# Two matmuls instead of three in each step of a recursive SwiGLU product, and weight sums made by DMA

## The chip, the cores and the metric

The kernel runs on one core of a Trainium2 chip. The metric is device time in microseconds (us) of one execution. Engines are named as in the profile: PE (matrix multiply), PEld (its weight loads), DVE (elementwise), ACT (activations and copies), POOL, and SP, whose queue issues most DMAs here.

## The reference, cut to what matters

One encoder layer on 512 tokens of width 2048, in float32: a gated linear attention mixer, a SwiGLU feed-forward block of width 5632, a gated input embedding and a last norm. The change touches only the first product of the feed-forward block:

```python
def swiglu(hn, w_in, w_out):
    gate, up = jnp.split(jnp.einsum('btd,de->bte', hn, w_in), 2, axis=-1)
    return jnp.einsum('btf,fd->btd', jax.nn.silu(gate) * up, w_out)
```

Here `w_in` is 2048 x 11264: 5632 columns of gate, then 5632 of up.

## The kernel before, in words

**Stages.** Activations lie with features on the 128 partitions and 512 tokens along the row. Four stages follow each other: the mixer (to about 714 us of the span), its output product (to 858 us), gate and up (864 to 1756 us), the down product and the embedding (to the end). All the large products run on PE in a split form: each float32 operand is cut into a high part (rounded by an ACT copy to the matmul type) and a low part (the rest, by a DVE subtraction), and a product is high by high, high by low and low by high, three matmuls that add into the same PSUM tile.

**Gate and up.** For each of 44 column tiles n (128 columns of gate and the 128 columns of up beside them) the kernel needs a 2 x 2 block product: weights a11, a12 (gate, upper and lower half of the 2048 input features) and a21, a22 (up), against two token halves of 256. It uses a seven-product recursive scheme: products p1, p2, p3, p4, q5, q6, p7, each of 8 steps of 128 features. The forms of the activations (`FM`) are made once. The forms of the weights are made for every n: a11, a12, a22 themselves, S3 = a11 + a21 for p7, s1 = a21 + a22 for q5, a11 + s1 for q6, and a12 + (a11 + s1) for p3. Results add up in three PSUM tiles, R1 (p1, q6, q5, p3), R2 (p2) and R7 (p7, p4); `combine` takes intermediate copies (v1, v2, v4) and builds gate `g` and up `u`, which are multiplied and written to memory by a DMA of POOL (`f_mid`).

**Order.** The stream for one n is p1(n), p3(n-1), p2(n), p7(n), q6(n), p4(n-1), q5(n). Raw weights are loaded (`Form.load`) five entries of the stream ahead, and a form is made (`Form.prep`: the sums, then high and low) two entries ahead. A scheduler then orders the instructions of each engine; each engine works through its own list in that order. High parts have three buffers, low parts three, raw weights six (`wr`): a load into one of these six has to wait until the last reader of what lay there is done.

**Names.** Every DVE and ACT operation is issued by one helper, line 70, so they are told apart by tiles: `w_hi` and `w_lo` are the parts of a form, `w_a` a raw weight tile, `w_s` (w_s3) the sum S3. Lines 724, 725 and 726 are the three matmuls, lines 123 to 125 the three matmuls of the other stages, line 676 the load of raw weights, line 761 the write of `f_mid`.

Of the kernel before, what the change touches and what calls it, by code (L numbers as in the profile page):

```python
# [9 lines left out]
F32 = mybir.dt.float32  # L10
F32R = mybir.dt.float32r
U8 = mybir.dt.uint8
AF = mybir.ActivationFunctionType
ALU = mybir.AluOpType

P = 128
T = 512
# [14 lines left out]
TH = T // 2  # L32
KH = KT // 2
# [4 lines left out]
def hybrid_kernel(ctx, tc, xT, pT, w_wide, w_lr, w_gu, b_gate, gla_norm, w_out,  # L38
                  mix_norm, ffn_norm, w_ffn_in, w_ffn_out, ple_norm, w_ple, fin_norm,
                  masks, resets, fold, outT):  # L40
    nc = tc.nc
    const = ctx.enter_context(tc.tile_pool(name="const", bufs=1))
    pp = ctx.enter_context(tc.tile_pool(name="pp", bufs=16))
    wp = ctx.enter_context(tc.tile_pool(name="wp", bufs=2))
# [4 lines left out]
    def f(ap):  # L49
        return ap.bitcast(F32)  # L50

    def bank(name):
        return mm_ps.tile([P, T], F32, name=name, tag="mm")
# [19 lines left out]
    vec = Counted(nc.vector, 60)  # L73
    act = Counted(nc.scalar, 100)
# [14 lines left out]
    WMAX = 8 * P  # L89

    class Block:
# [4 lines left out]
        def prep(self):  # L96
            if self.hi is not None:
                return
            n, m = self.n, self.m
            raw = wp.tile([P, WMAX], F32, name="w_raw", tag="raw", bufs=2)[:, : n * m]  # L100
            nc.sync.dma_start(raw.rearrange("p (k m) -> p k m", m=m), self.src)
            hi = wp.tile([P, WMAX], F32R, name="w_hi", tag="whi", bufs=3)[:, : n * m]
            lo = wp.tile([P, WMAX], F32R, name="w_lo", tag="wlo", bufs=3)[:, : n * m]
            act.activation(hi, raw, AF.Copy)
            vec.tensor_tensor(lo, raw, f(hi), ALU.subtract)
            self.hi = hi.rearrange("p (k m) -> p k m", m=m)
            self.lo = lo.rearrange("p (k m) -> p k m", m=m)
# [539 lines left out]
    rstd2 = wr = None  # L647
# [8 lines left out]
        out_ctx.close()  # L656
        wr = wr_ctx.enter_context(tc.tile_pool(name="wr", bufs=6))

    RAWS = {"p1": "a11", "p2": "a12", "p7": "a21", "q6": "a22"}
    FORM = {"p1": 1, "p2": 2, "p3": 3, "p4": 4, "q5": 5, "q6": 6, "p7": 7}  # L660
    pairs = {}

    class Form:
# [4 lines left out]
            self.w = pairs.setdefault(n, {})  # L668

        def load(self):  # L670
            name = RAWS.get(self.kind)
            if name is None or self.loaded or wr is None:
                return
            self.loaded = True
            t = wr.tile([P, WMAX], F32, name="w_a", tag="raw")
            nc.sync.dma_start(t.rearrange("p (k m) -> p k m", m=P), self.src(name))
            self.w[name] = t

        def prep(self):
            if self.hi is not None or wr is None:  # L680
                return
            self.load()
            w, kind = self.w, self.kind
            if kind == "p7":
                w["s3"] = wp.tile([P, WMAX], F32, name="w_s3", tag="raw", bufs=2)
                vec.tensor_tensor(w["s3"], w["a11"], w["a21"], ALU.add)
            elif kind == "q6":
                vec.tensor_tensor(w["a21"], w["a21"], w["a22"], ALU.add)
                vec.tensor_tensor(w["a11"], w["a11"], w["a21"], ALU.add)
            elif kind == "p3":  # L690
                vec.tensor_tensor(w["a12"], w["a12"], w["a11"], ALU.add)
            raw = w[{"p1": "a11", "p2": "a12", "p3": "a12", "p4": "a22", "q5": "a21", "q6": "a11", "p7": "s3"}[kind]]
            hi = wp.tile([P, WMAX], F32R, name="w_hi", tag="whi", bufs=3)
            lo = wp.tile([P, WMAX], F32R, name="w_lo", tag="wlo", bufs=3)
            act.activation(hi, raw, AF.Copy)
            vec.tensor_tensor(lo, raw, f(hi), ALU.subtract)
            self.hi = hi.rearrange("p (k m) -> p k m", m=P)
            self.lo = lo.rearrange("p (k m) -> p k m", m=P)
# [3 lines left out]
    def flush():  # L702
        while pending:
            pending.pop(0)()

    def product(b):
        b.prep()
        w, kind = b.w, b.kind
        if kind == "p1":
            w["R1"] = bank("ps_r1")  # L710
        elif kind == "p2":
            w["R2"] = bank("ps_r2")
        elif kind == "p7":
            w["R7"] = bank("ps_r7")
        ps = w[{"p2": "R2", "p7": "R7", "p4": "R7"}.get(kind, "R1")][:, 0:TH]
        fm = FM[FORM[kind]]
        fresh = kind in ("p1", "p2", "p7")
        if (b.n, kind) in ((0, "q5"), (FT - 1, "p3")):
            flush()
        for k in range(KH):  # L720
            xh, xl = fm[k][:, 0, :], fm[k][:, 1, :]
            ah, al = b.hi[:, k, :], b.lo[:, k, :]
            go = dict(skip_group_check=True)
            nc.tensor.matmul(ps, ah, xh, start=fresh and k == 0, stop=False, **go)  # L724
            nc.tensor.matmul(ps, ah, xl, start=False, stop=False, **go)  # L725
            nc.tensor.matmul(ps, al, xh, start=False, stop=k == KH - 1, **go)  # L726
        flush()
        pending.append(lambda: combine(b, ps))

    def temp(name):  # L730
        return pp.tile([P, T], F32, name=name, tag="res")

    A_T, B_T = slice(0, TH), slice(TH, T)

    def combine(b, ps):
        w, kind = b.w, b.kind
        if kind == "p1":
            w["v1"] = temp("v1")[:, A_T]
            act.activation(w["v1"], ps, AF.Copy)
        elif kind == "p2":  # L740
            g = w["g"] = temp("g")
            vec.tensor_tensor(g[:, A_T], ps, w["v1"], ALU.add)
            vec.tensor_tensor(g[:, A_T], g[:, A_T], rstd2[:, A_T], ALU.mult)
        elif kind == "q6":
            w["v2"] = temp("v2")[:, A_T]
            act.activation(w["v2"], ps, AF.Copy)
        elif kind == "q5":
            v4 = temp("v4")[:, A_T]
            act.activation(v4, ps, AF.Copy)
            w["u"] = temp("u")  # L750
            vec.tensor_tensor(w["u"][:, B_T], w["R7"][:, 0:TH], v4, ALU.subtract)
        elif kind == "p3":
            g = w["g"]
            vec.tensor_tensor(g[:, B_T], ps, rstd2[:, B_T], ALU.mult)
            act.activation(g, g, AF.Silu)
            vec.tensor_tensor(g, g, rstd2, ALU.mult)
        elif kind == "p4":
            u = w["u"]
            vec.tensor_tensor(u[:, A_T], ps, w["v2"], ALU.subtract)
            vec.tensor_tensor(u, u, w["g"], ALU.mult)  # L760
            nc.gpsimd.dma_start(Fd[b.n], u)
            pairs[b.n] = None
# [8 lines left out]
    for n in range(FT + 1):  # L771
        for kind, i in (("p1", n), ("p3", n - 1), ("p2", n), ("p7", n), ("q6", n), ("p4", n - 1), ("q5", n)):
            if 0 <= i < FT:
                stream.append((Form(i, kind, ffn_block(i)),
                               (lambda b: late_b(b)) if n == 0 else product))

    def late_b(b):

        product(b)
        at = ("p1", "p2", "p7", "q6").index(b.kind) if b.kind != "q5" else None  # L780
        if at is not None:
            for j in range(2 * at, 2 * at + 2):
                late_forms_b(j)
# [148 lines left out]
    for m in range(KT - LAST, KT):  # L932
        kept[m] = []
        for k0 in range(0, KT + PT, 4):
            k1 = min(k0 + 4, KT + PT)
            b = KeptBlock(ple_src(m, k0, k1), k1 - k0, P, "w")
# [90 lines left out]
    for m in range(KT - LAST, KT):  # L1027
        ps = bank("ps_hb")
# [91 lines left out]
```

## Time and profile before

| | us |
|---|---|
| median of 3 runs | 2457.65 (2456.04 to 2458.02) |
| the profiled execution | 2453.24 |
| its span, first to last instruction | 2451.4 |
| gate and up, in the span | 863.5 to 1756 |

The profile gives, for each engine, its busy time and, in the timeline, the start and length of each instruction. Lengths of matmuls overlap: the next one starts before the one before has left the array, so the rate is read from the distance between starts, not from the length. The same holds in a smaller way for DVE and ACT. "To landing" of a DMA is the time from its issue to its last byte.

### The profile page before, as it was taken

What the parts mean: (1) busy time and instruction counts of PE and PEld (TensorE: products, weight loads), DVE (VectorE), ACT (ScalarE), POOL (GpSimd) and SP (SyncE); (2) the same over time, 40 slices, a digit from 0 to 9 for tenths busy, and PEclk for the clock granted to TensorE, in tenths of its full rate; (3) what the DMA queues carried; (4) which work ended last, traced back from release to release, by engine and by line L of the source; (5) the groups of instructions that cost most, each with busy time, mean ns of one, the idle gap of its engine ahead of it and who ended that gap; (6) DMA issues with size and microseconds to landing.
All of it is one profiled execution on the core that took longest, in us unless ns stands there. A gap on an engine that the chain in (4) does not pass through costs nothing.

```text
span 2451.4 us, 35287 instructions
## 1 busy us (share of the span) xinstructions
PE 2410.5 (98%) x14428; PEld 2150.6 (88%) x14428; DVE 1596.6 (65%) x2220; ACT 1040.4 (42%) x1352; POOL 50.7 (2%) x102
## 2 busy tenths in 40 slices
PE   9999999999999999999999999999999999999997
PEld 6788887887888789999999999999888888888887
DVE  7595875856964487878787877878642422345445
ACT  5554644545543354444444444444431311234333
POOL 0000000000000000000000000000000000000000
PEclk9999999999999999999999999999999999999999
DMA  6222222222234243333333333333574644433333
GB/s 198 81 78 73 78 72 80 84 64 86 67 127 155 99 142 117 117 117 117 119 122 121 118 117 117 117 117 117 201 265 148 198 142 146 114 97 97 97 97 114
DMA packets 98099, 289.92 MB, mean 118 GB/s; under 512 B 12048, under 2 KB 17296, under 8 KB 97936
## 3 DMA queue, kind: packets, MB, share of 16 engines
q1 hardware_dynamic: 90576, 263.54, 34.3%
q0 software_dynamic: 7360, 24.12, 2.5%
q8 instruction: 113, 1.85, 0.3%
q14 instruction: 50, 0.41, 0.1%
HBM read 259.31 MB, written 28.31 MB: 117 GB/s over the span
## 4 chain that ended last, share of the span: by engine, by line
PE 95%; DVE 2%; ACT 2%; issue 1%; DMA 0%; SPq 0%; DVEq 0%; ACTq 0%
PE ps_r L724 12%; PE ps_r L725 12%; PE ps_r L726 12%; PE ps_dn L124 7%; PE ps_dn L125 7%; PE ps_dn L123 6%; PE ps_qk L123 2%; PE ps_qk L125 2%; PE ps_qk L124 2%; PE ps_out L124 2%; PE ps_og L123 2%; PE ps_out L125 2%; PE ps_out L123 2%; PE ps_og L124 2%; PE ps_og L125 2%; PE ps_pg L125 2%
## 5 line engine op out<-in xcount | busy, mean ns | idle before, releaser
L70 DVE TENSOR_TENSOR w_lo<-w_raw,w_hi 128x1024 fp32r<-128x1024 f32 (+2 forms) x271 | 306.4, 1131 | 352.2 <-ACT w_hi L70 351.8
L70 ACT ACTIVATE w_hi<-w_raw 128x1024 fp32r<-128x1024 f32 (+2 forms) x271 | 266.3, 983 | 613.2 <-PE ps_dn L124 303.7
L70 ACT ACTIVATE w_hi<-w_a 128x1024 fp32r<-128x1024 f32 x264 | 280.1, 1061 | 425.2 <-PE ps_r L725 298.4
L70 DVE TENSOR_TENSOR w_lo<-w_a,w_hi 128x1024 fp32r<-128x1024 f32 x264 | 322.4, 1222 | 104.7 <-ACT w_hi L70 98.5
L724 PE MATMUL ps_r<-fme,w_hi 128*128 128x256 f32 x1056 | 300.6, 285 | 5.2 <-issue 4.8
L725 PE MATMUL ps_r<-fme,w_hi 128*128 128x256 f32 x1056 | 300.3, 284 | 0.0
L726 PE MATMUL ps_r<-fme,w_lo 128*128 128x256 f32 x1056 | 299.9, 284 | 0.0
L123 PE MATMUL ps_dn<-hlf,w_hi 128*128 128x512 f32 x704 | 273.9, 390 | 1.6 <-ACT hlf L70 1.6
L124 PE MATMUL ps_dn<-hlf,w_hi 128*128 128x512 f32 x704 | 274.2, 389 | 0.4 <-DVE hlf L70 0.4
L125 PE MATMUL ps_dn<-hlf,w_lo 128*128 128x512 f32 x704 | 274.1, 389 | 0.0
L724 PEld LDWEIGHTS ps_r<-fme,w_hi 128*128 128x128 f32 x1056 | 204.1, 193 | 6.3 <-issue 5.6
L725 PEld LDWEIGHTS ps_r<-fme,w_hi 128*128 128x128 f32 x1056 | 204.1, 193 | 0.0
L726 PEld LDWEIGHTS ps_r<-fme,w_lo 128*128 128x128 f32 x1056 | 203.8, 193 | 0.0
L724 PE MATMUL ps_r<-fmb,w_hi 128*128 128x256 f32 x704 | 199.5, 283 | 1.3 <-ACT v L70 1.3
L724 PE MATMUL ps_r<-fma,w_hi 128*128 128x256 f32 x704 | 199.5, 283 | 0.0
L726 PE MATMUL ps_r<-fma,w_lo 128*128 128x256 f32 x704 | 199.4, 283 | 0.0
L725 PE MATMUL ps_r<-fmb,w_hi 128*128 128x256 f32 x704 | 199.4, 283 | 0.0
L725 PE MATMUL ps_r<-fma,w_hi 128*128 128x256 f32 x704 | 199.4, 283 | 0.0
L726 PE MATMUL ps_r<-fmb,w_lo 128*128 128x256 f32 x704 | 199.4, 283 | 0.0
L70 DVE TENSOR_TENSOR w_a<-w_a 128x1024 f32<-128x1024 f32 x132 | 160.9, 1219 | 20.6 <-DMA w_a<-in_w_ffn_in_dram 20.4
L123 PEld LDWEIGHTS ps_dn<-hlf,w_hi 128*128 128x128 f32 x704 | 132.1, 188 | 29.0 <-ACT hlf L70 1.8
L124 PEld LDWEIGHTS ps_dn<-hlf,w_hi 128*128 128x128 f32 x704 | 132.2, 188 | 28.2 <-DVE hlf L70 0.9
(244 smaller groups left out, 5089.1 us busy)
## 6 DMA issues: line engine op xcount, KB each, us to landing
w_a<-in_w_ffn_in_dram SPq DMA_DIRECT2D x176, 512.0 KB, 3.6
w_raw<-in_w_wide_dram SPq DMA_DIRECT2D x95, 512.0 KB, 3.5
w_raw<-in_w_ffn_out_dram SPq DMA_DIRECT2D x64, 512.0 KB, 3.7
w_raw<-in_w_ple_dram SPq DMA_DIRECT2D x42, 384.0 KB, 3.1
w_raw<-in_w_out_dram SPq DMA_DIRECT2D x24, 512.0 KB, 3.7
h<-h_mid SPq DMA_DIRECT2D x48, 256.0 KB, 3.8
w_raw<-in_w_ffn_out_dram SPq DMA_DIRECT2D x32, 384.0 KB, 3.2
f_mid<-u POOLq DMA_DIRECT2D x44, 256.0 KB, 3.6
```

Source lines behind the costliest of these rows:

```text
L70: return getattr(self.engine, op)(out, *args, **kw)
L123: nc.tensor.matmul(ps, ah, bh, start=first, stop=False)
L124: nc.tensor.matmul(ps, ah, bl, start=False, stop=False)
L125: nc.tensor.matmul(ps, al, bh, start=False, stop=last)
L724: nc.tensor.matmul(ps, ah, xh, start=fresh and k == 0, stop=False, **go)
L725: nc.tensor.matmul(ps, ah, xl, start=False, stop=False, **go)
L726: nc.tensor.matmul(ps, al, xh, start=False, stop=k == KH - 1, **go)
```

## The change: 512 columns at once, and sums by DMA

High by high and high by low have the same weights (the high part), and the high and low part of the activations lie side by side. The two matmuls of 256 columns become one of 512, into both halves of the PSUM tile; low by high is added into the second half. So the wanted value is the sum of the two halves, and `combine` now works on 512 columns and adds the halves at the end (`merge`; in p3 an ACT copy and a DVE addition). Two of the four weight sums, S3 and s1, are no longer added by DVE: a plain load brings the first summand and a second DMA, issued by POOL, adds the other one into the same tile. For this a11, a21 and a22 are read from memory twice. S3 lies in the two-buffer pool that held it before; s1, a11, a12 and a22 share the six.

```diff
-    RAWS = {"p1": "a11", "p2": "a12", "p7": "a21", "q6": "a22"}
+    RAWS = {"p1": ("a11",), "p2": ("a12",), "p7": ("a21", "a11"), "q6": ("a21", "a22"), "p4": ("a22",)}
+    KEEP = {"p1": "a11", "p2": "a12", "p7": "s3", "q6": "s1", "p4": "a22"}
+    SPLIT = {"p1": "a11", "p2": "a12", "p3": "a12", "p4": "a22", "q5": "s1", "q6": "a11", "p7": "s3"}
...
-            t = wr.tile([P, WMAX], F32, name="w_a", tag="raw")
-            nc.sync.dma_start(t.rearrange("p (k m) -> p k m", m=P), self.src(name))
-            self.w[name] = t
+            pool, bufs = (wp, 2) if self.kind == "p7" else (wr, 6)
+            t = pool.tile([P, WMAX], F32, name="w_a", tag="raw", bufs=bufs)
+            nc.sync.dma_start(t, self.src(names[0]).rearrange("p k m -> p (k m)"))
+            for more in names[1:]:
+                nc.gpsimd.dma_start(t, self.src(more).rearrange("p k m -> p (k m)"), accum_op=ALU.add)
+            self.w[KEEP[self.kind]] = t
...
-            if kind == "p7":
-                w["s3"] = wp.tile([P, WMAX], F32, name="w_s3", tag="raw", bufs=2)
-                vec.tensor_tensor(w["s3"], w["a11"], w["a21"], ALU.add)
-            elif kind == "q6":
-                vec.tensor_tensor(w["a21"], w["a21"], w["a22"], ALU.add)
-                vec.tensor_tensor(w["a11"], w["a11"], w["a21"], ALU.add)
+            if kind == "q6":
+                vec.tensor_tensor(w["a11"], w["a11"], w["s1"], ALU.add)
...
-            nc.tensor.matmul(ps, ah, xh, start=fresh and k == 0, stop=False, **go)
-            nc.tensor.matmul(ps, ah, xl, start=False, stop=False, **go)
-            nc.tensor.matmul(ps, al, xh, start=False, stop=k == KH - 1, **go)
+            nc.tensor.matmul(ps, b.hi[:, k, :], fm[k].rearrange("p a x -> p (a x)"),
+                             start=fresh and k == 0, stop=False, **go)
+            nc.tensor.matmul(ps[:, TH:T], b.lo[:, k, :], fm[k][:, 0, :], start=False, stop=k == KH - 1, **go)
...
+    def merge(out, t):
+        vec.tensor_tensor(out, t[:, A_T], t[:, B_T], ALU.add)
...
         if kind == "p1":
-            w["v1"] = temp("v1")[:, A_T]
+            w["v1"] = temp("v1")
             act.activation(w["v1"], ps, AF.Copy)
         elif kind == "p2":
             g = w["g"] = temp("g")
-            vec.tensor_tensor(g[:, A_T], ps, w["v1"], ALU.add)
-            vec.tensor_tensor(g[:, A_T], g[:, A_T], rstd2[:, A_T], ALU.mult)
+            vec.tensor_tensor(w["v1"], ps, w["v1"], ALU.add)
+            merge(g[:, A_T], w["v1"])
...
-            vec.tensor_tensor(w["u"][:, B_T], w["R7"][:, 0:TH], v4, ALU.subtract)
+            vec.tensor_tensor(v4, w["R7"], v4, ALU.subtract)
+            merge(w["u"][:, B_T], v4)
         elif kind == "p3":
             g = w["g"]
-            vec.tensor_tensor(g[:, B_T], ps, rstd2[:, B_T], ALU.mult)
+            act.activation(g[:, B_T], ps[:, B_T], AF.Copy)
+            vec.tensor_tensor(g[:, B_T], ps[:, A_T], g[:, B_T], ALU.add)
+            vec.tensor_tensor(g, g, rstd2, ALU.mult)
             act.activation(g, g, AF.Silu)
             vec.tensor_tensor(g, g, rstd2, ALU.mult)
         elif kind == "p4":
             u = w["u"]
-            vec.tensor_tensor(u[:, A_T], ps, w["v2"], ALU.subtract)
+            vec.tensor_tensor(w["v2"], ps, w["v2"], ALU.subtract)
+            merge(u[:, A_T], w["v2"])
```

On PE, at the start of p1 of column tile 22, two of the eight steps stood like this before (ps_r1 is R1, fme a form of the activations):

```order
L724 MATMUL ps_r1_11646<-fme_5615,w_hi_11578 128x256
L725 MATMUL ps_r1_11646<-fme_5615,w_hi_11578 128x256
L726 MATMUL ps_r1_11646<-fme_5615,w_lo_11579 128x256
L724 MATMUL ps_r1_11646<-fme_5615,w_hi_11578 128x256
L725 MATMUL ps_r1_11646<-fme_5615,w_hi_11578 128x256
L726 MATMUL ps_r1_11646<-fme_5615,w_lo_11579 128x256
```

And with the change (two steps and the first matmul pair of the next, which has another tile of forms):

```order
L724 MATMUL ps_r1_10538<-fme_5615,w_hi_10482 128x512
L726 MATMUL ps_r1_10538<-fme_5615,w_lo_10483 128x256
L724 MATMUL ps_r1_10538<-fme_5615,w_hi_10482 128x512
L726 MATMUL ps_r1_10538<-fme_5615,w_lo_10483 128x256
L724 MATMUL ps_r1_10538<-fme_5828,w_hi_10482 128x512
L726 MATMUL ps_r1_10538<-fme_5828,w_lo_10483 128x256
```

A step is one matmul of 512 columns and one of 256 instead of three of 256; the order of the products is the same.

On DVE, from the low part of p1(22) to the low part of q6(22), the list before reads (w_a_11478 is a11 of tile 22, 11576 a21, 11608 a22, 11546 a12, w_s3 the sum S3; 11317 is a12 of tile 21):

```order
L70 TENSOR_TENSOR w_lo_11579<-w_a_11478,w_hi_11578 128x1024
L70 TENSOR_TENSOR w_a_11576<-w_a_11576,w_a_11608 128x1024
L70 TENSOR_TENSOR u_11444<-ps_r7_11289,v2_11377 128x256
L70 TENSOR_TENSOR w_lo_11612<-w_a_11317,w_hi_11611 128x1024
L70 TENSOR_TENSOR u_11444<-u_11444,g_11314 128x512
L70 TENSOR_TENSOR w_a_11478<-w_a_11478,w_a_11576 128x1024
L70 TENSOR_TENSOR w_lo_11643<-w_a_11546,w_hi_11642 128x1024
L70 TENSOR_TENSOR u_11673<-ps_r7_11518,v4_11671 128x256
L70 TENSOR_TENSOR w_a_11546<-w_a_11546,w_a_11478 128x1024
L70 TENSOR_TENSOR w_lo_11678<-w_s3_11675,w_hi_11677 128x1024
L70 TENSOR_TENSOR g_11543<-ps_r1_11417,rstd2_6615 128x256
L70 TENSOR_TENSOR w_lo_11712<-w_a_11478,w_hi_11711 128x1024
```

With the change the same stretch reads (w_a_10404 is a11 of tile 22, 10504 the loaded and added s1, 10479 S3, 10457 a12, 10279 a12 of tile 21):

```order
L70 TENSOR_TENSOR w_lo_10483<-w_a_10404,w_hi_10482 128x1024
L70 TENSOR_TENSOR w_a_10404<-w_a_10404,w_a_10504 128x1024
L70 TENSOR_TENSOR v2_10324<-ps_r7_10259,v2_10324 128x512
L70 TENSOR_TENSOR w_lo_10509<-w_a_10279,w_hi_10508 128x1024
L70 TENSOR_TENSOR u_10379<-v2_10324 128x256
L70 TENSOR_TENSOR u_10379<-u_10379,g_10276 128x512
L70 TENSOR_TENSOR w_lo_10535<-w_a_10457,w_hi_10534 128x1024
L70 TENSOR_TENSOR v4_10555<-ps_r7_10437,v4_10555 128x512
L70 TENSOR_TENSOR w_a_10457<-w_a_10457,w_a_10404 128x1024
L70 TENSOR_TENSOR u_10557<-v4_10555 128x256
L70 TENSOR_TENSOR w_lo_10561<-w_a_10479,w_hi_10560 128x1024
L70 TENSOR_TENSOR w_lo_10586<-w_a_10404,w_hi_10585 128x1024
```

The sum for q6 (second row) stands where the sum s1 stood, and reads the tile that the adding DMA fills; the low part of q6 (last row) is the last reader of a11, and in the six-buffer rotation the tile s1 of column tile 23 takes the place of a11 of tile 22.

On POOL, around the write of tile 21, only writes stood before:

```order
L761 DMA f_mid20_134<-u_11444 128x512
L761 DMA f_mid21_135<-u_11673 128x512
L761 DMA f_mid22_136<-u_11902 128x512
```

and with the change (10835 is S3 of tile 24, 10682 is s1 of tile 23, 11013 S3 of 25, 10860 s1 of 24; the L682 rows are adding DMAs):

```order
L769 DMA f_mid20_134<-u_10379 128x512
L682 DMA w_a_10835<-in_w_ffn_in_dram 128x1024
L682 DMA w_a_10682<-in_w_ffn_in_dram 128x1024
L769 DMA f_mid21_135<-u_10557 128x512
L682 DMA w_a_11013<-in_w_ffn_in_dram 128x1024
L682 DMA w_a_10860<-in_w_ffn_in_dram 128x1024
```

Two adding DMAs come between two writes: first S3, loaded nearly two column tiles ahead of its use, then s1, one tile ahead.

## Rows read from the trace of the kernel before

**Rows 1.** Busy time in stretches: PE, PEld, DVE, ACT, POOL, then clock, DMA share, GB/s.
```profile
863.50:1756.00 892.50, 890.45 (x7392) 889.55 (x7392) 714.20 (x800) 388.76 (x488) 23.21 (x43) 1.00 0.35 119
1000.00:1400.00 400.00, 400.00 (x3336) 400.00 (x3335) 319.57 (x359) 173.44 (x219) 10.80 (x20) 1.00 0.35 118
```

**Rows 2.** The chain that ended last, shares of the span by engine.
```profile
PE 95%; DVE 2%; ACT 2%; issue 1%; DMA 0%; SPq 0%; DVEq 0%; ACTq 0%
```

**Rows 3.** Timeline of PE in gate and up: start, length, instruction.
```profile
1199.77 0.28 PE L726 MATMUL ps_r<-fmb,w_lo 128*128 128x256 f32 x1
...
1208.89 0.28 PE L724 MATMUL ps_r<-fmb,w_hi 128*128 128x256 f32 x1
```

**Rows 4.** Timeline of PE in the down product, 512 columns.
```profile
1849.69 0.39 PE L125 MATMUL ps_dn<-hlf,w_lo 128*128 128x512 f32 x1
...
1855.81 0.39 PE L125 MATMUL ps_dn<-hlf,w_lo 128*128 128x512 f32 x1
```

**Rows 5.** Timeline of DVE in gate and up.
```profile
1204.57 0.68 DVE L70 TENSOR_TENSOR u<-u,g 128x512 f32<-128x512 f32 x1
1205.17 1.22 DVE L70 TENSOR_TENSOR w_a<-w_a 128x1024 f32<-128x1024 f32 x1
1206.30 1.22 DVE L70 TENSOR_TENSOR w_lo<-w_a,w_hi 128x1024 fp32r<-128x1024 f32 x1
1207.44 0.42 DVE L70 TENSOR_TENSOR u<-ps_r,v 128x256 f32<-128x256 f32 x1
1207.77 1.22 DVE L70 TENSOR_TENSOR w_a<-w_a 128x1024 f32<-128x1024 f32 x1
...
1212.69 0.42 DVE L70 TENSOR_TENSOR g<-ps_r,v 128x256 f32<-128x256 f32 x1
1213.15 0.42 DVE L70 TENSOR_TENSOR g<-g,rstd 128x256 f32<-128x256 f32 x1
```

**Rows 6.** Groups by line, DVE, 1000 to 1400 us; then count, busy, mean ns, idle before.
```profile
L70 DVE TENSOR_TENSOR w_lo<-w_a,w_hi 128x1024 fp32r<-128x1024 f32 x119 | 145.4, 1222 | 47.9 <-ACT w_hi L70 45.0
L70 DVE TENSOR_TENSOR w_a<-w_a 128x1024 f32<-128x1024 f32 x60 | 73.1, 1219 | 9.9 <-DMA w_a<-in_w_ffn_in_dram 9.8
L70 DVE TENSOR_TENSOR w_s<-w_a 128x1024 f32<-128x1024 f32 x20 | 24.5, 1226 | 13.6 <-DMA w_a<-in_w_ffn_in_dram 13.6
```

**Rows 7.** The same view of DVE in the down product: 512 columns from PSUM.
```profile
L70 DVE TENSOR_TENSOR h<-ps_dn,h 128x512 f32<-128x512 f32 x48 | 33.1, 691 | 127.1 <-PE ps_dn L125 127.1
```

**Rows 8.** The same view of ACT: gate and up, then 512 columns from PSUM (mixer).
```profile
L70 ACT ACTIVATE w_hi<-w_a 128x1024 fp32r<-128x1024 f32 x120 | 127.3, 1061 | 197.1 <-PE ps_r L725 139.2 <-issue 58.0
L70 ACT ACTIVATE v<-ps_r 128x256 f32<-128x256 f32 x59 | 21.6, 366 | 0.0
L70 ACT ACTIVATE Ov<-ps_o 128x512 f32<-128x512 f32 x16 | 9.6, 598 | 26.9 <-PE ps_o L125 26.9
```

**Rows 9.** Waits of SP's DMA queue, 1000 to 1400 us: total, times, longest.
```profile
SPq L676 <- DVE w_lo L70: 370.6, 80, 8.2
```

**Rows 10.** DMA queues and issues, 863 to 1756 us; the last row is of the whole span.
```profile
q1 hardware_dynamic: 26329, 94.29, 31.9%
w_a<-in_w_ffn_in_dram SPq DMA_DIRECT2D x170, 512.0 KB, 3.6
f_mid<-u POOLq DMA_DIRECT2D x43, 256.0 KB, 3.6
h_mid<-h POOLq DMA_DIRECT2D x32, 256.0 KB, 2.3
```

**Rows 11.** Timeline at the start of gate and up: SP, PE, DVE.
```profile
858.23 37.39 SPq L676 DMA_DIRECT2D w_a<-in_w_ffn_in_dram  x12
...
864.67 0.58 PE L724 MATMUL ps_r<-fme,w_hi 128*128 128x256 f32 x1 [0.39 <-ACT w_hi L70]
...
868.67 0.41 PE L724 MATMUL ps_r<-fme,w_hi 128*128 128x256 f32 x1
868.89 0.42 PE L725 MATMUL ps_r<-fme,w_hi 128*128 128x256 f32 x1
...
865.79 1.22 DVE L70 TENSOR_TENSOR w_s<-w_a 128x1024 f32<-128x1024 f32 x1
```

**Rows 12.** Timeline of DVE at the end of gate and up.
```profile
1755.69 0.42 DVE L70 TENSOR_TENSOR u<-ps_r,v 128x256 f32<-128x256 f32 x1
1756.15 0.69 DVE L70 TENSOR_TENSOR u<-u,g 128x512 f32<-128x512 f32 x1
```

## What the change will do to the time: the prediction, written before the changed kernel had run

> **What bounds the kernel now.** I read the stretches first. In gate and up PE is busy for 400.00 of 400.00 us in the middle, DVE for 320, ACT for 173, and the DMA engines for 0.35; the granted clock is 1.00, the upper level of 2.4 GHz [rows 1]. The chain that ends last says the same for the whole span: PE 95%, DVE and ACT 2% each [rows 2]. So what PE needs per column tile sets the time of this stage, and everything else counts only where it makes PE wait. The view that gives PE's price is the timeline: 76 steps from one start to the next, 1199.77 to 1208.89, are 9.12 us, so a matmul of 256 columns costs 0.1200 us, although its row says 0.28 [rows 3]. In the down product 27 such steps of 512 columns, 1849.69 to 1855.81, are 6.12 us: 0.2267 us each [rows 4]. The difference, 0.1067 us, is the price of 256 columns; what is left in either, 0.0133 us, is paid once per matmul. The waits of the other engines show where the slack is thin. DVE stands idle until a raw weight's DMA has landed for 13.6 us before the 20 sums S3 and 9.8 us before the other sums, in 400 us [rows 6], and SP's queue waits for a low part before each of its 80 loads, 371 us in all [rows 9]: loads start when a buffer comes free and land just in time.
>
> **PE's part.** Per step, three matmuls of 256 (0.3600 us) become one of 512 and one of 256 (0.2267 + 0.1200 = 0.3467 us). There are 7392 matmuls in the stage [rows 1], 2464 steps; 2464 x 0.0133 = 32.9 us saved. A column tile of 56 steps goes from 20.16 to 19.41 us. Below this it can't go, as no column is saved and the other stages have their old matmuls. No row mixes both widths; if the fixed part were paid otherwise, the saving is between 0 and 32.9 us, and I take 32.9 since both widths show the same 0.0133.
>
> **DVE's part.** From one start to the next 1024 columns take 1.13 us (1205.17 to 1206.30), 512 take 0.60 (1204.57 to 1205.17), 256 take 0.33 (1207.44 to 1207.77), and 0.46 where the next reads the result (1212.69 to 1213.15) [rows 5]. From PSUM 512 columns are as long as from SBUF, 691 against 680 ns [rows 5, 7]. Per tile before: 7 low parts, 4 sums, 2 of 512 and 5 of 256: 11 x 1.13 + 2 x 0.60 + 5 x 0.33 = 15.3 us. After: 7 low parts, 2 sums, 6 of 512 and 4 of 256: 10.2 + 3.6 + 1.3 = 15.1 us of 19.41. The wider `combine` eats what the two sums give back, so DVE stays covered by PE.
>
> **ACT's part.** Three copies grow from 0.37 to 0.60 us and one of 256 is added [rows 8]: 9.1 becomes 10.2 us per tile, also covered.
>
> **The adding DMAs.** Instead of 4 loads of 512 KB a tile has 5 on SP and 2 that add on POOL. The queue of SP moved 94.29 MB in 31.9% of 893 us, 331 GB/s while busy [rows 10], so 512 KB are 1.6 us of data, and the 3.6 us to landing contain 2.0 us that are fixed. The trace has no adding DMA. Let Y be its time from POOL's issue to landing. Nearest rows: a plain 512 KB load, 3.6 us; POOL's writes of 256 KB, 2.3 and 3.6 us, of which 0.8 is data, so 1.5 to 2.8 fixed [rows 10]. If the add costs no more than a load, Y is 3.6 us. If the two summands pass one after the other it is 2.0 to 2.8 + 3.2 = 5.2 to 6.0 us. The far end is three passes and the other adding DMA wholly ahead of it in the queue: 2.8 + 2 x 4.7 = 12.2 us. The least price for PE is nothing, not a gain, since the sums on DVE were not on its path.
>
> What Y may be comes from a loop. The load of s1 for tile n+1 takes the buffer of a11(n), free when the low part of q6(n) is made. Then: load 3.6 us, adding DMA Y, and on DVE the sum for q6(n+1), which waits for it, with all that is queued behind it up to the low part of q6(n+1): six of 1024, three of 512 and two of 256 columns: 6.8 + 1.8 + 0.7, plus 0.2 for the one dependence and the full length of the last, 9.5 us. The loop lasts 13.1 + Y. Queued behind the wait are the low parts of p3(n), p2, p7 and q6, and PE waits for the first of them; POOL's write of f_mid stands behind the adding DMAs too, but that is read much later. PE needs 19.41 us per tile, so the loop is hidden while Y is below 6.3 us. Rows with 3.6 and the estimate of 5.2 to 6.0 lie under that, and I take Y near 5.5: hidden, with little to spare. S3 has nearly two tiles of lead and is hidden anyway, except that its adding DMA stands ahead of s1's in POOL's queue. The data to move rise from 4.5 to 7.5 pieces of 512 KB per tile, at 1.6 us 12 us of 19.41, or 15 us if the adds count double: the DMA engines are busier, not full.
>
> **The edges.** At the start SP issues its loads from 858.23; PE runs at 0.21 to 0.22 us per 256 columns at first (868.67 to 868.89, twice 0.1067 us: the level of 1.2 GHz), and the third raw tile is there at 865.79 at the latest [rows 11]. The adding DMA for s1(0) then lands at 869.4 to 872, and sum, high and low part of q6 (1.1 + 1.1 + 1.2 us) are ready at 873 to 875.5; p1 at the lower clock and p2 and p7 at 2.9 us end at about 875. I take 1.0 us of loss. At the end the last subtraction of 256 columns (0.46 us to the next, 1755.69 to 1756.15 [rows 12]) becomes one of 512 and a merge: 0.6 us more.
>
> **The sum.** -32.9 + 1.0 + 0.6 = -31.3 us on the profiled execution's 2453.24, 2422. That execution lies 4.4 us below the median of the runs, 2457.65; set against the median the forecast is 2426 us. Its own range, with the startup from 0 to 4 us and single late adds, is 2421 to 2434.
>
> **Rivals.**
> *The loop becomes the bound.* If the two summands pass one after the other, S3's adding DMA ahead in the queue holds s1's back as well: in the loop the low parts of p7 and q6 are 1.13 us apart, so 3.2 - 1.1 = 2.1 us are added to 5.2, Y = 7.3, the loop is 20.4 us, and 44 x (20.4 - 19.41) = 44 us go on top of 2426: 2470. Each us of Y beyond 6.3 costs 44 us; from Y = 7.0 on the kernel is slower than before, and the far end, 12.2 us, is 2685. For it: the DVE list puts the waiting sum ahead of the low part of p3, DVE already waits for plain loads [rows 6], and a second DMA now stands in series with them. Against it: the fixed part of a POOL write can be as low as 1.5 us, and in step with PE the two low parts are about one product, 2.8 us, apart, so the queue adds only 0.4.
> The Trainium skill (Collectives: The Full Stack, section on the bandwidth ceiling and the fold count) says that a reducing transfer runs at about half the rate of a copy because it reads two sources through the same ring; no row here shows one. By that rule this rival's doubled data time holds, and its 2470 with it.
> *The change doesn't do what it says on PE.* The 0.0133 us could belong to the switch of what streams through the array, or to the second half of the tile being added to, so that a step of 512 and 256 again takes 0.36 us: then the kernel stays at 2458 to 2460. For it speaks only that no row mixes widths; against it, that two widths give the same rest [rows 3, 4].
> *The start or the end costs far more,* by PE falling to its lower clock again while s1(0) is awaited: some 10 us lost per 5 us of gap at the start, which would only shrink the gain, and with a longer gap undo it: 2440 to 2465.
>
> **How the numbers follow.** PE stays the bound: 0.53. The loop decides: 0.36, of which 0.05 still ends faster (Y 6.3 to 6.9), 0.05 within 0.2%, 0.26 slower. No gain on PE: 0.08, half within 0.2% and half slower through DMA waits. The start: 0.03, counted as slower. 0.2%, 4.9 us, is about what a measurement of this kernel can tell from no change. Faster 0.58, same 0.09, slower 0.33. The predicted time is that of the likeliest case. The range starts at 2420, as PE can't save more, and goes up to 2500 (Y = 8.0), which leaves out about 0.15 of the chance above.
>
> **What would show it.** Right: matmul starts in gate and up at 0.2267 and 0.1200 us in turn, the stage 861 us long, PE busy throughout, the sum for q6 waiting less than 1.7 us for its DMA, and adding DMAs that land in under 6.3 us. Wrong: PE waiting for the low part of p3 once per tile, DVE idle before the sum of q6 for several us with an adding DMA as the releaser, tiles 20 us or more apart; or steps that still take 0.36 us.

## The result: slower by 8.6%, because the loop of s1 became the bound

The changed kernel takes 2668.68 us (median of 4 runs, 2665.03 to 2671.76) against 2457.12 in 4 runs of before beside it: ratio 1.0861, 95% interval 1.0842 to 1.0879. The forecast was 2426, with a range to 2500. Its profiled execution took 2665.03 us, its span 2663.0.

The stretches after (columns as in [rows 1]); gate and up now ends at about 1970 us:

```profile
863.50:1970.00 1106.50, 954.46 (x4938) 819.79 (x4939) 705.95 (x853) 437.98 (x547) 99.13 (x130) 0.91 0.60 160
1000.00:1400.00 400.00, 344.57 (x1781) 296.18 (x1780) 250.60 (x303) 154.19 (x192) 36.69 (x48) 0.91 0.59 158
```

No engine is full any more: PE is busy for 345 of 400 us where it was 400, DVE for 251 where it was 320, and the DMA share is 0.59, not 1. Something is being waited for in a circle. Between the first and the last write of f_mid in that stretch a column tile takes 25.09 us (20.18 before); 43 x 4.91 us = 211 us is the whole loss. The chain that ended last, by engine, to compare with [rows 2]:

```profile
PE 61%; DMA 22%; DVE 10%; ACT 3%; issue 3%; POOL 0%; POOLq 0%; DVEq 0%; SPq 0%; ACTq 0%
```

DMA was 0% in it. The same chain in order of time (start, length, what):

```profile
1216.03 1.07 ACT w_hi L70
1217.12 1.23 DVE w_lo L70
1218.37 4.76 DMA w_a<-in_w_ffn_in_dram
1223.16 0.04 POOLq L682
1223.20 0.49 issue
1223.69 10.31 DMA w_a<-in_w_ffn_in_dram
1234.05 0.04 issue
1234.09 1.23 DVE w_a L70
1235.32 0.60 DVE v L70
1235.92 1.14 DVE w_lo L70
1237.06 0.04 issue
1237.11 0.58 PE ps_r L726
```

These rows lie inside one tile, and they are the circle: the low part of q6 frees a11's buffer, the plain load of the next s1 takes 4.76 us, POOL issues the adding DMA, which takes 10.31 us, DVE's sum for q6 waits for it, and PE waits for the low part of p3 that stands behind the sum. DVE's list then leads to the next low part of q6, which closes the circle. The timeline of DVE shows the same from its side:

```profile
1208.71 1.23 DVE L70 TENSOR_TENSOR w_a<-w_a 128x1024 f32<-128x1024 f32 x1 [6.14 <-DMA w_a<-in_w_ffn_in_dram]
...
1215.86 2.49 DVE L70 TENSOR_TENSOR w_lo<-w_a,w_hi 128x1024 fp32r<-128x1024 f32 x2
...
1234.09 1.23 DVE L70 TENSOR_TENSOR w_a<-w_a 128x1024 f32<-128x1024 f32 x1 [7.22 <-DMA w_a<-in_w_ffn_in_dram]
```

From the sum (1208.71) to the end of q6's low part (1218.35) are 9.6 us, from there to the next sum 15.7: 25.4 us. The mean of the 16 tiles between 1000 and 1400 us is 9.9 us for DVE's half, 5.3 for the plain load with POOL's issue and 9.9 from there to the sum, 9.8 of it the adding DMA (8.3 to 10.6): together 25.1, the tile. The sums of DVE, 1000 to 1400 us, beside [rows 6], and the waits of PE in the whole of gate and up (total, times, longest):

```profile
L70 DVE TENSOR_TENSOR w_a<-w_a 128x1024 f32<-128x1024 f32 x32 | 39.1, 1221 | 108.4 <-DMA w_a<-in_w_ffn_in_dram 108.4
```
```profile
PE ps_r L726 <- DVE w_lo L70: 142.5, 44, 4.6
```

Before these sums DVE's wait for the DMA was 9.8 us in all at 60 of them (and 13.6 us at the 20 sums S3), and is 108.4 us at 32. PE waits 44 times for a low part, once per column tile, 3.2 us each. It stands idle for 152 of the 1106.5 us (2 of 892.5 before), and the granted clock falls after each of these stalls and is 0.91 in the stretch, 1.00 before. The slower steps are mostly a consequence of the stalls and not a second cause: the circle runs over DMAs and DVE. They reach into it only where PE, still at the low clock, makes ACT late with q6's high part and DVE waits for that, 4.7 us in the 16 tiles, 0.3 us each. The DMA view, 1000 to 1400 us, beside [rows 10]:

```profile
q1 hardware_dynamic: 11496, 41.85, 33.3%
q0 software_dynamic: 5888, 20.97, 25.8%
...
w_a<-in_w_ffn_in_dram SPq DMA_DIRECT2D x80, 512.0 KB, 4.7
w_a<-in_w_ffn_in_dram POOLq DMA_DIRECT2D x32, 512.0 KB, 9.0
```

An adding DMA lands after 9.0 us in the median, where the forecast took 5.5, and a plain load after 4.7 instead of 3.6. Why they take so long is seen when the circle is cut into short stretches (columns of [rows 1]; the last but one is the DMA share):

```profile
1208.70:1218.40 9.70, 6.81 (x30) 5.78 (x30) 9.61 (x12) 2.70 (x4) 0.58 (x1) 0.82 0.26 88
1218.40:1234.10 15.70, 14.90 (x85) 12.68 (x83) 6.14 (x9) 7.90 (x10) 1.70 (x2) 1.00 0.77 198
```
```profile
1224.00:1226.00 2.00, 2.00 (x13) 1.77 (x12) 0.41 (x2) 1.44 (x2) 0.53 (x1) 1.00 0.94 186
1226.00:1228.00 2.00, 2.00 (x14) 1.72 (x13) 0.88 (x1) 0.76 (x2) 0.00 (x0) 1.00 1.06 252
1228.00:1230.00 2.00, 2.00 (x14) 1.72 (x13) 0.00 (x0) 0.40 (x1) 0.00 (x0) 1.00 1.00 256
1230.00:1232.00 2.00, 2.00 (x13) 1.77 (x12) 0.00 (x0) 1.54 (x2) 0.00 (x0) 1.00 0.88 211
1232.00:1234.00 2.00, 1.30 (x8) 0.84 (x6) 0.00 (x0) 1.01 (x2) 0.00 (x0) 1.00 0.11 27
1234.00:1237.00 3.00, 0.00 (x0) 0.00 (x0) 2.91 (x4) 0.53 (x2) 0.00 (x0) 0.80 0.00 0
```

The first two rows are the two halves of the circle. While DVE does its 9.6 us the DMA share is 0.26 (2.5 us of work), while the transfers run it is 0.77 (12.1 us). The mean of 0.59 hides a burst: for the first 6 of the 10.3 us of s1's adding DMA the engines are full (0.94 to 1.06), and when it has landed nothing moves. The burst slows plain loads as well. The DMA view of the loads issued from 1210 to 1218 us, ahead of it, and of the four transfers issued from 1220 to 1225:

```profile
w_a<-in_w_ffn_in_dram SPq DMA_DIRECT2D x2, 512.0 KB, 3.7
```
```profile
w_a<-in_w_ffn_in_dram SPq DMA_DIRECT2D x2, 512.0 KB, 9.3
w_a<-in_w_ffn_in_dram POOLq DMA_DIRECT2D x2, 512.0 KB, 9.6
```

The two slow loads are on SP's queue, not behind the adds in POOL's. At the forecast's prices two loads and two adds are 2 x 1.6 + 2 x 3.2 = 9.6 us of data (an estimate), and all four take about that, 8.9 to 10.3, whichever queue they are on. Between 1000 and 1400 us the 31 loads that overlap an add by more than 3 us took 8.6 us in the median, the 32 that overlap none 3.7.

### The profile page after: what moved, and what is told of

Read it like the earlier page. It is cut to its first block, busy times and chain, and to the rows that moved or that the text cites. A ratio compares the mean times of both kernels' runs of the same rounds, so it can differ in the third digit from the quotient of the medians.

```text
span 2663.0 us, 30763 instructions
## 1 busy us (share of the span) xinstructions
PE 2477.9 (93%) x11964; PEld 2083.0 (78%) x11964; DVE 1580.7 (59%) x2264; ACT 1080.0 (41%) x1396; POOL 127.9 (5%) x190
## 4 chain that ended last, share of the span: by engine, by line
PE 61%; DMA 22%; DVE 10%; ACT 3%; issue 3%; POOL 0%; POOLq 0%; DVEq 0%; SPq 0%; ACTq 0%
DMA w_a<-in_w_ffn_in_dram 22%; PE ps_dn L124 6%; PE ps_dn L125 6%; PE ps_dn L123 6%; PE ps_r L724 5%; DVE w_lo L70 5%; PE ps_r L726 3%; PE ps_qk L123 2%; PE ps_og L123 2%; PE ps_og L125 2%; PE ps_qk L124 2%; PE ps_qk L125 2%; PE ps_og L124 2%; PE ps_out L125 2%; PE ps_out L123 2%
## 5 line engine op out<-in xcount | busy, mean ns | idle before, releaser
L70 DVE TENSOR_TENSOR w_lo<-w_a,w_hi 128x1024 fp32r<-128x1024 f32 x308 | 375.0, 1221 | 107.3 <-ACT w_hi L70 106.4
L724 PE MATMUL ps_r<-fme,w_hi 128*128 128x512 f32 x1056 | 381.3, 402 | 4.6 <-issue 4.4
L724 PE MATMUL ps_r<-fmb,w_hi 128*128 128x512 f32 x704 | 313.5, 469 | 1.5 <-ACT v L70 1.5
L726 PEld LDWEIGHTS ps_r<-fmb,w_lo 128*128 128x128 f32 x704 | 167.4, 238 | 154.6 <-DVE w_lo L70 154.6
L70 DVE TENSOR_TENSOR w_a<-w_a 128x1024 f32<-128x1024 f32 x88 | 107.3, 1221 | 285.5 <-DMA w_a<-in_w_ffn_in_dram 285.5
L724 PE MATMUL ps_r<-fma,w_hi 128*128 128x512 f32 x704 | 249.7, 395 | 1.2 <-ACT w_hi L70 1.2
L724 PEld LDWEIGHTS ps_r<-fme,w_hi 128*128 128x128 f32 x1056 | 203.9, 193 | 54.8 <-issue 5.9
L724 PEld LDWEIGHTS ps_r<-fmb,w_hi 128*128 128x128 f32 x704 | 164.9, 234 | 41.4 <-ACT v L70 1.8
L724 PEld LDWEIGHTS ps_r<-fma,w_hi 128*128 128x128 f32 x704 | 132.1, 188 | 31.9 <-ACT w_hi L70 1.5
L125 PEld LDWEIGHTS ps_dn<-hlf,w_lo 128*128 128x128 f32 x704 | 132.9, 189 | 27.5
```

The source lines that it names most:

```text
L70: return getattr(self.engine, op)(out, *args, **kw)
L125: nc.tensor.matmul(ps, al, bh, start=False, stop=last)
L724: nc.tensor.matmul(ps, b.hi[:, k, :], fm[k].rearrange("p a x -> p (a x)"), start=fresh and k == 0, stop=False, **go)
L726: nc.tensor.matmul(ps[:, TH:T], b.lo[:, k, :], fm[k][:, 0, :], start=False, stop=k == KH - 1, **go)
```

## The experiments

Times are medians, "tile" is the mean distance of the writes of f_mid between 1000 and 1400 us, "landing" the median of POOL's transfers of 512 KB there.

| run | time, us | ratio to before (95%) | tile, us | landing, us |
|---|---|---|---|---|
| changed kernel | 2668.68 | 1.0861 (1.0842 to 1.0879) | 25.09 | 9.0 |
| e1 matmuls alone | 2453.84 | 0.9992 (0.9983 to 1.0002) | 19.99 | |
| e2 own buffers | 2443.97 | 0.9944 (0.9923 to 0.9965) | 19.76 | 7.7 |
| e3 without S3's add | 2597.94 | 1.0570 (1.0554 to 1.0586) | 23.55 | 8.6 |
| e4 plain instead of adding | 2542.30 | 1.0348 (1.0333 to 1.0364) | 22.19 | 7.2 |
| e5 e2, wide matmuls first | 2438.49 | 0.9931 (0.9918 to 0.9945) | 19.53 | 7.2 |
| e6 adds alone | 2602.23 | 1.0590 (1.0569 to 1.0611) | 23.51 | 8.4 |
| e7 without a22's load, 5 buffers | 2594.22 (one run) | | 22.96 | 7.4 |
| e8 only S3 by DMA | 2542.26 | 1.0348 (1.0334 to 1.0362) | 22.33 | 8.2 |
| e9 e3 and e4 together | 2484.35 (one run) | | 20.75 | 5.8 |
| e10 e2, shorter lookahead | 2434.71 | 0.9914 (0.9900 to 0.9927) | 19.42 | 7.6 |
| e11 e5, first tile by DVE | 2434.67 | 0.9914 (0.9900 to 0.9928) | 19.54 | 7.1 |
| e12 e1, wide matmuls first | 2457.26 | 1.0008 (0.9999 to 1.0017) | 20.18 | |

### e1: the wide matmul and its combine, all sums by DVE

```diff
-    RAWS = {..., "p7": ("a21", "a11"), "q6": ("a21", "a22"), "p4": ("a22",)}
+    RAWS = {..., "p7": ("a21",), "q6": ("a22",)}
...
```

> The wide matmul and its wider combine alone: S3 and s1 are added by DVE as before, from four plain loads per tile. Theory A (the loop through the adding DMA of s1 is the whole loss, 25.4 us per tile): PE is the bound again and the time is under 2457 us. How far under tells what a step of 512 and 256 costs: at 0.3467 us per step 2426, at the 0.354 us per step seen in the trace of the changed kernel about 2441. Theory B (the wider combine on DVE and ACT, or the adds into half of the PSUM tile, is what costs): the time stays well above 2457, DVE being busy for 17.4 us of a tile.

No change in time. None of the 8.6% is in this half, but it doesn't earn its 33 us either. The groups of DVE in 1000 to 1400 us, those that wait:

```profile
L70 DVE TENSOR_TENSOR w_a<-w_a 128x1024 f32<-128x1024 f32 x60 | 73.2, 1219 | 10.0 <-DMA w_a<-in_w_ffn_in_dram 10.0
L70 DVE TENSOR_TENSOR g<-g,rstd 128x512 f32<-128x512 f32 x40 | 27.5, 689 | 0.7
L70 DVE TENSOR_TENSOR w_s<-w_a 128x1024 f32<-128x1024 f32 x20 | 24.5, 1226 | 35.4 <-DMA w_a<-in_w_ffn_in_dram 35.4
```

DVE is busy for 353.99 us there, and with these waits (10.0 + 0.7 + 35.4) that is 400: DVE has no slack left. With four sums kept, the wide `combine` brings its work to 17.7 us of a tile of 20, and its waits for loads fill the rest. The work alone would fit under the 19.41 of PE.

### e2: the whole change, the six buffers given out by kind (a11 1, a12 2, s1 2, a22 1)

```diff
-    LOADS = 5
+    LOADS = 12
...
-            pool, bufs = (wp, 2) if self.kind == "p7" else (wr, 6)
+            own = {"p1": 1, "p2": 2, "q6": 2, "p4": 1}
+            pool, bufs = (wp, 2) if self.kind == "p7" else (wr, own[self.kind])
+            tag = "raw" if self.kind == "p7" else self.kind
...
```

> All of the change is kept, both adding DMAs too; the six raw buffers are only given out differently: one for a11, two for a12, two for s1, one for a22, instead of in turn. So s1 of tile n no longer waits for the low part of q6(n-1) but for that of q5(n-2), some 22 us ahead of its use instead of 16. Theory A (the loop): 5.4 us load and 10.4 us adding DMA fit into the lead, and the time falls to that of the wide matmul alone, 2426 to 2445. Theory C (the adding DMAs slow the core as such, by the traffic of the DMA engines or by POOL beside DVE): it stays above 2550.

The same adds, bytes, the same six buffers: 225 us less, because s1's next load no longer waits for a11 (loads are also put further ahead here; e10 takes that out again). The same stretch:

```profile
1000.00:1400.00 400.00, 400.00 (x2266) 347.00 (x2265) 320.01 (x386) 195.65 (x243) 46.57 (x61) 1.00 0.75 200
```

PE is full again, at a DMA share of 0.75, higher than in the slow kernel. So the adds' traffic as such doesn't slow the kernel. The ten runs fall into two clusters, five at 2433.66 to 2437.99 and five at 2449.95 to 2451.66; e10 shows a difference of that size.

### e3 and e4: one adding DMA left out, or both made plain

e3 leaves out the second transfer of S3, e4 lets both second transfers overwrite instead of add, so each leaves summands out. First e3, then e4:

```diff
-            for more in names[1:]:
+            for more in names[1:] if self.kind == "q6" else ():
```
```diff
-                nc.gpsimd.dma_start(t, self.src(more).rearrange("p k m -> p (k m)"), accum_op=ALU.add)
+                nc.gpsimd.dma_start(t, self.src(more).rearrange("p k m -> p (k m)"))
```

> The adding DMA of S3 is left out (S3 is then a21 alone); that of s1 stays, in the same place of the loop. If the 10.4 us of s1's adding DMA are mostly waiting behind that of S3 in POOL's queue, it falls to 5.3 to 6.2 us as for the lone ones at the start of the stage, the loop to 9.5 + 4.5 + 6 = 20 us per tile, and the time to about 2440 to 2470. If an adding DMA takes 9 to 10 us here by itself because of the plain loads beside it, the time stays above 2620.

> The two second transfers of each tile stay on POOL's queue with the same waits, but overwrite instead of add (S3 and s1 are then their second summand alone). If the adding is what makes them slow (two operands read), they land in about 4 us, or 5 with the queue, the loop is 9.5 + 4.5 + 5 = 19 us and the time 2426 to 2450. If POOL's queue as such is slow for 512 KB, they still take 8 us or more and the time stays above 2550.

Both came out between the two numbers given, so each theory had part of it: without S3's add the tile is 1.54 us shorter, without the adding itself 2.90, and even plain transfers on POOL's queue land in 7.2 us. That left open what these 7.2 are.

### e9: both cuts at once

```diff
+            for more in names[1:] if self.kind == "q6" else ():
+                nc.gpsimd.dma_start(t, self.src(more).rearrange("p k m -> p (k m)"))
```

> The changed kernel without the second transfer of S3, and with a second transfer of s1 that overwrites instead of adding (both sums are wrong). Theory of the burst (the transfers that are set free together share the DMA engines; an add costs more of them than a plain transfer): what the two cuts saved one by one adds up, 25.09 - 1.54 - 2.90 = 20.65 us per column tile, about 2475 us, and s1's second transfer lands in 5.5 to 6 us. Rival (a transfer of 512 KB on POOL's queue takes 7 us by itself): it still lands in 7.2 us, the loop is 9.5 + 5 + 7.2 = 21.7 us, 2520 us.

The tile is 20.75 us (20.65 expected), and s1's second transfer, alone on its queue and plain, lands in 5.8:

```profile
w_a<-in_w_ffn_in_dram SPq DMA_DIRECT2D x96, 512.0 KB, 4.5
w_a<-in_w_ffn_in_dram POOLq DMA_DIRECT2D x20, 512.0 KB, 5.8
```

The four kernels make a square: leaving out S3's transfer saves 1.54 us of the tile with adding and 1.44 without, adding costs 2.90 us with S3's and 2.80 without. The costs add up, and the rival (7 us by itself) is out. That they add up fits a shared full resource, but fits one queue as well; against the queue speak the slow loads of SP in the burst above. s1's second transfer alone lands, in the mean of its tiles from 1000 to 1400 us, in 9.8 us in the changed kernel, 8.3 in e3, 7.3 in e4 and 5.9 in e9.

### e6: the adds alone, with the three matmuls and the combine of before

Against the changed kernel, the matmuls (the combine of before stands behind them):

```diff
-            nc.tensor.matmul(ps, b.hi[:, k, :], fm[k].rearrange("p a x -> p (a x)"),
+            nc.tensor.matmul(ps, ah, xh, start=fresh and k == 0, stop=False, **go)
+            nc.tensor.matmul(ps, ah, xl, start=False, stop=False, **go)
...
```

> The three matmuls and the combine of before, with the two sums made by adding DMAs in the buffers of the changed kernel. Loop theory: the loop per column tile is the DVE part, shorter than the 9.5 us of the changed kernel by the four combine operations that lie in it (about 1.2 us), so 8.3 to 8.7, and the two transfers of s1, 5.4 + 10.3 us: 24.0 to 24.4 us, the time 2620 to 2640 us. Rival (the wide combine on DVE is what makes the sums late, the adds alone are hidden): within 10 us of the 2456 of before. Rival (all of the loss is the adds', whatever DVE does): 2670 us or more, tile 25 us.

Somewhat better than expected, but a loop of the kind expected:

```profile
1218.82 1.23 DVE L70 TENSOR_TENSOR w_a<-w_a 128x1024 f32<-128x1024 f32 x1 [4.04 <-DMA w_a<-in_w_ffn_in_dram]
...
1226.23 1.22 DVE L70 TENSOR_TENSOR w_lo<-w_a,w_hi 128x1024 fp32r<-128x1024 f32 x1
```

From the sum to the end of q6's low part DVE needs 8.6 us, as worked out; the rest of the 23.51, 14.9 us, is the two transfers, 0.8 less than expected. The adds alone make the kernel slow.

### e8: only S3 by an adding DMA, s1 again added by DVE

```diff
+    RAWS = {..., "p7": ("a21", "a11"), "q6": ("a21",)}
...
+            if self.kind == "q6":
+                self.w["a22"] = wr.tile([P, WMAX], F32, name="w_a", tag="raw", bufs=6)
+                nc.sync.dma_start(self.w["a22"], self.src("a22").rearrange("p k m -> p (k m)"))
...
+                vec.tensor_tensor(w["s1"], w["s1"], w["a22"], ALU.add)
```

> Only S3 is formed by an adding DMA; s1 is again loaded as a21 and a22 and added by DVE. Loop theory: S3 is loaded nearly two tiles ahead in a pool of its own and its add is in no loop, so it costs nothing however long it takes: 2437 to 2455 us, tile 19.4 to 20.0 us, bound by PE (and DVE at some 17 us per tile). Rival (an adding DMA slows or delays the other transfers by its traffic and its queue): tile above 20.5 us, 2480 us or more.

The forecast of this run was wrong: 22.33 us per tile, where the rival had above 20.5. What binds is a circle that I had not looked for, through the load of a22 (first SP, then DVE):

```profile
1210.54 0.33 SPq L686 DMA_DIRECT2D w_a<-in_w_ffn_in_dram  x1
```
```profile
1209.29 2.35 DVE L70 TENSOR_TENSOR w_lo<-w_a,w_hi 128x1024 fp32r<-128x1024 f32 x2
...
1217.48 1.22 DVE L70 TENSOR_TENSOR w_a<-w_a 128x1024 f32<-128x1024 f32 x1 [5.83 <-DMA w_a<-in_w_ffn_in_dram]
...
1231.63 1.22 DVE L70 TENSOR_TENSOR w_lo<-w_a,w_hi 128x1024 fp32r<-128x1024 f32 x1
```

With the new order of loads a22 takes the buffer of s1 of the tile before, is issued when q5's low part is done (1210.54), and the sum s1 waits for it until 1217.48. From that sum to the next low part of q5 (1231.63 + 1.2) are 15.4 us, and 6.9 for the load: 22.3. A plain load does here what the adding DMA did above. But S3's add is not out of it: a22's load is issued while that add and the load of a21 are in flight. The DMA view of what is issued from 1207.3 to 1211 us:

```profile
w_a<-in_w_ffn_in_dram SPq DMA_DIRECT2D x2, 512.0 KB, 7.0
w_a<-in_w_ffn_in_dram POOLq DMA_DIRECT2D x1, 512.0 KB, 7.9
```

The median load of SP here takes 4.3 us, and with that the circle would be 19.7 (an estimate). What the add and what the second load have of the difference, no run separates, so the rival stands in part.

### e7: a run that tests another kernel than its expectation

```diff
+    RAWS = {..., "p7": ("a21", "a11"), "q6": ("a21", "a22")}
+    SPLIT = {..., "p4": "s1", "q5": "s1", "q6": "a11", "p7": "s3"}
...
+            pool, bufs = (wp, 2) if self.kind == "p7" else (wr, 5)
```

> Leaves out the second transfer of S3, and the second transfer of s1 overwrites instead of adding (both sums are wrong). Theory of the burst (the transfers that are set free together share the DMA engines, and the adding costs about 3 us on top): the two cuts add up, 25.09 - 1.54 - 2.90 = 20.65 us per tile, near 2476 us; s1's second transfer lands in about 5.5 us. Rival (a transfer of POOL's queue takes 7 us by itself): it still lands in 7 us, tile 22 us, 2540 us.

Under this label ran not that kernel but one that left out the load of a22 (p4 is computed with s1's weights) and had five shared buffers; the kernel that is described here is e9. In the one that ran, s1's next load waits for the low part of p4, which reads the s1 of the tile before, instead of that of q6, so it has a circle of its own, and its 22.96 us per tile decide nothing.

### e5, e10, e11, e12: what the change is worth without the loop

e5 is e2 with the eight wide matmuls of a product first and the eight narrow ones behind them, from tile 1 on:

```diff
...
+            for k in range(KH):
+                wide(k)
+            for k in range(KH):
+                narrow(k)
...
```

> The kernel of the own buffers, and from column tile 1 on the eight 512-column matmuls of a product stand first and its eight 256-column ones behind them. Theory (the two rates of a step, 0.3467 and 0.3533 us, come from the alternation of wide and narrow matmuls): eight steps take 8 x (0.2267 + 0.1200) = 2.77 us in every run, the tile 19.4 us, all runs between 2430 and 2440 us, and no second cluster near 2451. Rival (the rates come with the step, in whatever order): the runs fall into two clusters near 2435 and 2451, as with the own buffers alone, 16 us apart = 2464 steps x 0.0067 us.

No second cluster: 2437.54 to 2443.01, one run of five above the 2440; the tile is 0.1 us above the 19.4. That the alternation causes the two rates isn't shown by it, as the four runs of e10, which alternate, have no second cluster either. e10 is e2 with the lookahead of the changed kernel (`LOADS = 5`):

> The own buffers by kind, with loads only five entries ahead as in the changed kernel. Loop theory (the tile was set by s1's next load waiting for a11's buffer, so the buffers alone undo it): tile 19.4 to 19.9 us, 2433 to 2455 us. Rival (what helped in the own-buffers kernel was that loads were put twelve entries ahead): tile above 21 us, 2500 us or more.

The buffers alone undo the loss. Its steps, first and last of 16 starts of a wide matmul, then the same of e2's profiled execution (2451.13 us, of the slower cluster):

```profile
1199.73 0.39 PE L726 MATMUL ps_r<-fma,w_hi 128*128 128x512 f32 x1
...
1204.93 0.39 PE L726 MATMUL ps_r<-fmb,w_hi 128*128 128x512 f32 x1
```
```profile
1199.85 0.40 PE L726 MATMUL ps_r<-fme,w_hi 128*128 128x512 f32 x1
...
1205.15 0.40 PE L726 MATMUL ps_r<-fmb,w_hi 128*128 128x512 f32 x1
```

15 steps in 5.20 us, 0.3467 each, the forecast's number to the digit, against 5.30 us, 0.3533. 2464 x 0.0067 = 16 us is about the distance of e2's clusters (no run of its faster cluster was profiled). What chooses between the two rates stays open.

e11 is e5 with s1 of column tile 0 loaded as two tiles and added by DVE:

```diff
...
+            if kind == "q6" and self.n == 0:
+                vec.tensor_tensor(w["s1"], w["s1"], w["a22"], ALU.add)
...
```

> Own buffers, wide matmuls first, and in column tile 0 alone s1 is loaded as two tiles and added by DVE. Theory (at the start of gate and up the sum of q6 waits 4 to 5 us for the adding DMA of s1, and PE with it): 3 to 8 us less than the 2438.5 of the same kernel without this, 2430 to 2436 us. Rival (the start is set by the forms of the activations and the clock, not by s1): 2436 to 2441 us, no change.

3.8 us better than e5, at the lower end of the 3 to 8: the first sum for q6 starts at 872.02 instead of 875.89. First e5, then e11:

```profile
875.89 1.23 DVE L70 TENSOR_TENSOR w_a<-w_a 128x1024 f32<-128x1024 f32 x1 [3.69 <-DMA w_a<-in_w_ffn_in_dram]
```
```profile
872.02 1.22 DVE L70 TENSOR_TENSOR w_a<-w_a 128x1024 f32<-128x1024 f32 x1
```

The intervals of the two ratios just overlap, so the 3.8 is rough. e12 is e1 with the matmuls in the order of e5:

> The wide matmul and its combine alone, all sums by DVE, with the eight wide matmuls of a product first and the eight narrow ones behind them. Theory (the matmuls alone gave only 19.99 us per tile because their steps took 0.3508 us; the order fixes them near 0.349 and the rest were waits for DVE, busy 17.7 us of a tile): tile 19.6 to 19.8 us, 2440 to 2448 us; the adds with buffers of their own are then worth 2 to 10 us. Rival (DVE's load sets the tile without the adds): tile 19.9 us or more, 2450 us or more, and the adds are worth 12 us.

The rival was right: DVE's 352.51 us busy and its waits for loads fill the 400 again, the tile is 20.18 us, and in the six shared buffers the wide matmuls alone are worth nothing. The adds and the buffers by kind together are worth 19 us (e1 to e10, e12 to e5). No run has such buffers without the adds; as part of what fills DVE's time in e1 and e12 are waits for loads, how much of the 19 us needs the adds stays open. e10 and e11 are both 0.86% faster than before, 21 us.

## Why the prediction was wrong

**PE's part** was right where PE is the bound: 0.3467 us per step in e10, though a second rate of 0.3533 occurs. The rival that a step stays at 0.36 is out.

**DVE's and ACT's part** were covered, as said, where the loop doesn't bind (e10: PE busy 400 of 400 us, DVE 325). With all sums on DVE it has no slack left (e1).

**The loop** was named rightly: its members, its order and DVE's share (9.5 us forecast, 9.9 measured) are the rows above. The price for it holds too: 44 x (25.09 - 19.41) = 250 us on top of 2426 are 2676, and 2669 was measured. PE waits once per tile for the low part of p3, DVE for the adding DMA before q6's sum, and tiles are 25 us apart, as the signs for "wrong" had it.

**The failed step is the size of Y, and with it of the plain load before it.** "I take Y near 5.5" was 9.8 in the mean, and "load 3.6 us" was 5.3 with POOL's issue, so that Y would have had to stay under 4.6 to be hidden, not under 6.3. In the place of 13.1 + 5.5 = 18.6 stand 9.9 + 5.3 + 9.9 = 25.1. By the square, the 9.8 are made of these: 5.9 a plain transfer on POOL's queue beside SP's loads, where the rows of before gave 3.6; about 2.4 the adding, where the forecast had 1.6 for a doubled data time; about 1.5 S3's transfer, where the rival of the loop had 2.1. (Of the 2.90 us that the adding costs per tile, most of the rest is in DVE's half.) That rival had the right circle, and the low parts of p7 and q6 back to back as it said (1215.86, two in 2.49 us), but with Y = 7.3 too small a size: it left the loads of SP out, which move at the same time. Its far end, 12.2 us, lies beyond what happened.

Adding costs nearly double the data time: while busy, POOL's queue moved 20.97 MB in 25.8% of 400 us, 203 GB/s, with adds, and with the same transfers made plain (e4, below) 23.60 MB in 16.2%, 364 GB/s.

```profile
q0 software_dynamic: 6624, 23.60, 16.2%
```

The Trainium skill (Collectives: The Full Stack, section on the bandwidth ceiling and the fold count) has the reducing step of a ring collective at half the rate of the copying one, as the add needs two source reads; the ratio of 1.8 here, for an adding DMA and with f_mid's writes included, is near that. The kernel's time would be 2470 by that rule in the forecast; it is 2669, since the larger part of Y is not the adding.

**Why 3.6 was the wrong row.** It was the landing time in a kernel whose loads came one by one, at a DMA share of 0.35. The change frees s1's, S3's, a22's and a11's buffers within the few us of DVE's low parts, so their transfers run as one burst at a share near 1, in which the plain loads too take 9.3 us. The forecast had the sum, "12 us of 19.41, or 15 us if the adds count double", and set it against the whole tile. They are 14.6 us in the two halves above. But 12.1 of them are set free by the last low parts and move between that and the next sum, and in a tile of 19.41 us DVE's half leaves 9.8 for that: they do not fit. In e2 and e10 the same bytes flow all the time, an add lands in 7.6 to 7.7 us, and PE doesn't wait, because s1 has two buffers of its own and is loaded earlier.

**The edges** were small beside this. In e5 the first sum for q6 waits 3.7 us for its DMA, and e11 got 3.8 us back; 1.0 was forecast. In the trace of e1 the last output matmul ends 3 us later than before with the same instructions on PE ahead of it: the granted clock was 0.97 between 100 and 200 us, 1.00 in before.

## What to carry to other kernels

When an edit puts a second transfer in series into a buffer that rotates, write down the circle (last reader, load, second transfer, first reader) and price its transfers at the traffic that the circle itself releases, not at the landing time of a calm trace. Share out the bytes over the part of the period in which they can move, not over all of it. And where a circle binds, give the one tensor in it a second buffer of its own before giving the idea up: here the same six buffers, dealt by kind, turned +8.6% into -0.86%. A plain load can close such a circle as well (e8).

## What was not expected of the hardware

- Alternating matmuls of 512 and 256 columns run at 0.3467 or at 0.3533 us per pair, at a granted clock of 1.00 in both: e10 held the first and e2's profiled execution the second wherever I measured, e1 changes between them.
- A plain 512 KB transfer on POOL's queue, the only one of that size there, landed in 5.8 us beside SP's 4.5 (e9); POOL's writes of 256 KB, 2.3 to 3.6 us before, took 7.3 us behind an add in e10.
- In the changed kernel plain 512 KB loads of SP's queue took 3.7 us ahead of the burst and 9.3 us in it, beside two adding DMAs: a queue of their own did not protect them.
